# Layer 0's down end reordered, three k/v products placed into it, and half of the row scaling moved from the projection into the attention

## The chip, the cores and the metric

The kernel runs on one core of a Trainium2 chip. The core has a matrix engine (TensorE, PE in the profile; PEld is its weight load), a vector engine (VectorE, DVE), an engine for activations (ScalarE, ACT), a general one (GpSimd, POOL) and one that mostly issues transfers (SyncE, SP). Each works through its own queue of instructions in order; semaphores hold an instruction until what it needs is there. The metric is the device time of one execution in microseconds (us).

## The reference, cut to what matters

A stream of 1024 latent tokens and 256 context tokens of width 1024 goes through two layers, each a mixer and a gated convolutional FFN; after both, `x <- LayerNorm(alpha*x + gate*f)`. Layer 0's FFN ends with a product with w_down; layer 1's mixer is attention in a window of 128 tokens to each side and over the context, with 16 query heads and 2 key/value heads.

```python
def odd_project(h, w_in):
    q, k, v = jnp.split(h @ w_in, [C_Q, C_Q + C_KV], axis=-1)
    return heads(q, C_HEADS), heads(k, C_KV_HEADS), heads(v, C_KV_HEADS)

def odd_mixer(h_lat, h_ctx, w_in, w_out, sink, cos, sin, ctx_out):
    q, k, v = odd_project(h_lat, w_in)
    qc, kc, vc = odd_project(h_ctx, w_in)
    q = apply_rope(q, cos, sin)
    k = apply_rope(k, cos, sin)
    y, yc = window_gqa_sink(q, k, v, qc, kc, vc, sink, ctx_out)
    return y @ w_out, ((yc @ w_out) if ctx_out else None)
```

The layer norm between them is split in the kernel: rows are centred and divided by their deviation at once; gain and bias are folded into the modulation that the projection needs, and are put on the stored rows ("row scaling") later, since only the residual at the mixer's end reads them.

## The kernel before, in words

Products are made in three parts (high times high, high times low, low times high) from operands split into a rounded high part and a rest; `mm3` issues the three matmuls (L401 to L403). `split` makes the parts of a weight: ACT casts (L112), DVE or POOL subtracts (L113).

**The down end** (`ffn2`, then `finish_l` in `run`). The product with w_down for columns 512 to 1023 runs with one PSUM bank (`d0` to `d7`) for each of the eight rows of 128 tokens. The last six of its pairs of inputs (18 matmuls) are done row by row. When row t's bank is complete, DVE multiplies by the gate (`tt`, L2039), adds to `z` (L1977) and takes statistics (L1978, L357); POOL takes the root (`rs`, L359, L360); DVE makes `nmr` (L2778), ACT scales `z` (L2779). One row later come eight transposes of `z` (L384) into `d(t-1)` and `d(t)`, eight evictions on ACT with the modulation (`hst`, L390), and on DVE a cast to the high part and a subtraction for the low one (L395, L396). The order on every engine is the program's there.

**The projection** (`l1_project`). First the k/v columns (256) of the eight rows, then the q columns 0 to 511 (q0 phase) and 512 to 1023 (q1 phase), 24 matmuls each. Between rows of the q0 phase the two context rows are normalised, turned (into `tr` banks, pool `pt1`) and projected. Each q row is rotated (L436, L446 on DVE, L450 on POOL), and two products later turned (L471) and evicted, high by ACT (L461), low by DVE (L462), then stored to `qC0`/`qC1`; k likewise to `kC`. In each q row, `sum_rows` also makes part of the next modulation vectors: a load (`accr`), a split (`ahl`, L321, L322), two matmuls (L325, L326) and an addition (`abr`, L330). And `scale_rows` (L2475 to L2478) scales half a row: SP loads 512 columns of a row of x2 into `xs`, DVE multiplies and adds, POOL issues the store. PE's order is the program's (`manual_pe`); the order on the other engines is set by the scheduler.

**The attention** (`attn_c`). Thirty-two groups of four heads and 128 queries, two units each. A unit makes scores `S` (L762), DVE adds the mask and takes the row bound (L2654), ACT exponentiates (L783), POOL divides (L786) by what DVE inverted (L785); PE turns the result `P` (`T`, L858), ACT and DVE copy it out (L773, L771), and PE multiplies with v (`pv`, L867). A dictionary of side jobs (`side`) runs a job with the loads of a group, such as a piece of w_out (`out_weight`: L1215, L1216).

## Time and profile before

| what | us |
|---|---|
| median of 3 runs | 2911.86 (2909.92 to 2914.53) |
| the profiled execution | 2915.36 |
| its span in the trace | 2913.5 |
| mean granted PE clock in it | 0.979 |
| down product, its last rows | about 1707 to 1756 |
| projection of layer 1 | about 1766 to 1908 |
| attention of layer 1 | 1908 to about 2145 |

The places are read off the timeline, from the start of the span. A row of the timeline gives start, duration, engine, line, operation, output and inputs, and in brackets the idle time of the engine before it and what ended that. A row of the table of windows gives, for a stretch of time, each engine's busy time with its number of instructions, and the granted clock of PE as a share of full speed.

### The profile page before, as it was taken

What the parts mean: (1) busy time and instruction counts of PE and PEld (TensorE: products, weight loads), DVE (VectorE), ACT (ScalarE), POOL (GpSimd) and SP (SyncE); (2) the same over time, 40 slices, a digit from 0 to 9 for tenths busy, and PEclk for the clock granted to TensorE, in tenths of its full rate; (3) what the DMA queues carried; (4) which work ended last, traced back from release to release, by engine and by line L of the source; (5) the groups of instructions that cost most, each with busy time, mean ns of one, the idle gap of its engine ahead of it and who ended that gap; (6) DMA issues with size and microseconds to landing.
All of it is one profiled execution on the core that took longest, in us unless ns stands there. A gap on an engine that the chain in (4) does not pass through costs nothing.

```text
span 2913.5 us, 45188 instructions
## 1 busy us (share of the span) xinstructions
PE 2761.8 (95%) x16596; PEld 2251.1 (77%) x16596; DVE 2139.0 (73%) x3832; ACT 1382.7 (47%) x2598; POOL 691.7 (24%) x968
## 2 busy tenths in 40 slices
PE   6989999999999999999999998989999899999997
PEld 4877777777789987888888877766677788888886
DVE  4876366667588778888877656557778888888778
ACT  3221155567535654455553343257753555555541
POOL 2610143354451000000001013435544011111002
PEclk8999999999999999999999999999999999999999
DMA  8468721033558653333367525732234455555862
GB/s 262 138 186 272 214 66 34 17 104 116 156 154 245 213 177 104 105 118 111 117 218 286 177 80 192 235 105 63 71 119 155 140 173 167 173 166 206 325 218 93
DMA packets 370517, 456.87 MB, mean 157 GB/s; under 512 B 26152, under 2 KB 265032, under 8 KB 368760
## 3 DMA queue, kind: packets, MB, share of 16 engines
q1 hardware_dynamic: 342808, 369.40, 40.5%
q0 software_dynamic: 24592, 82.89, 8.2%
q8 instruction: 130, 2.13, 0.3%
q10 hardware_dynamic: 2896, 1.70, 0.2%
q14 instruction: 91, 0.75, 0.1%
HBM read 337.98 MB, written 115.93 MB: 156 GB/s over the span
## 4 chain that ended last, share of the span: by engine, by line
PE 67%; DVE 10%; issue 10%; DMA 7%; ACT 4%; POOL 1%; SPq 0%; ACTq 0%; DVEq 0%; POOLq 0%
PE q L1704 8%; PE x L1704 7%; PE y L1704 7%; PE S L762 5%; PE v L1704 4%; PE pv L907 3%; PE T L893 3%; PE dy L2365 3%; PE mm L401 3%; PE mm L402 2%; PE mm L403 2%; PE d L401 2%; PE d L402 2%; PE d L403 2%; PE dx L2365 2%
## 5 line engine op out<-in xcount | busy, mean ns | idle before, releaser
L786 POOL TENSOR_SCALAR P<-P,rin 128x640 f32<-128x640 f32 (+3 forms) x288 | 250.9, 876 | 344.3 <-DVE rin L785 321.3
L1678 DVE TENSOR_TENSOR w<-raw,w 128x512 fp32r<-128x512 f32 x308 | 209.6, 694 | 85.6 <-ACT w L1676 85.5
L112 ACT CAST w<-raw 128x512 fp32r<-128x512 f32 x315 | 183.4, 621 | 173.4 <-PE d L403 61.1
L113 DVE TENSOR_TENSOR w<-raw,w 128x512 fp32r<-128x512 f32 x299 | 194.3, 689 | 70.3 <-ACT w L112 68.3
L762 PE MATMUL S<-k,q 64*128 64x256 f32 (+2 forms) x1824 | 192.4, 337 | 17.1 <-DVE nm L2654 8.1
L783 ACT ACTIVATE P<-P,nm 128x641 f32<-128x641 f32 (+4 forms) x208 | 161.3, 777 | 82.5 <-DVE nm L2654 46.7
L1676 ACT CAST w<-raw 128x512 fp32r<-128x512 f32 x308 | 182.1, 621 | 15.1 <-DVE raw L1683 10.1
L762 PEld LDWEIGHTS S<-k,q 64*128 64x128 f32 x1824 | 136.0, 188 | 52.7 <-issue 18.3
L773 ACT COPY PT<-T 128x512 f32<-128x512 f32 (+1 forms) x250 | 134.1, 566 | 77.9 <-PE T L893 75.8
L907 PE MATMUL pv<-PT,v 128*64 128x128 f32 x2016 | 133.4, 280 | 16.7 <-ACT PT L773 14.3
L893 PE MATMUL T<-ident,P 128*128 128x128 f32 x1008 | 136.7, 282 | 6.8 <-POOL P L786 2.3
L907 PEld LDWEIGHTS pv<-PT,v 128*64 128x64 f32 x2016 | 109.3, 138 | 42.6 <-ACT PT L773 23.2
L401 PE MATMUL d<-w,w 128*128 128x512 f32 x352 | 138.0, 392 | 0.0
L402 PE MATMUL d<-w,w 128*128 128x512 f32 x352 | 137.4, 390 | 0.0
L403 PE MATMUL d<-w,w 128*128 128x512 f32 x352 | 137.3, 390 | 0.0
L785 DVE RECIPROCAL rin<-den 128x1 f32<-128x1 f32 x288 | 46.1, 162 | 118.7 <-ACT P L783 116.1
L771 DVE COPY PT<-T 128x512 f32<-128x512 f32 (+1 forms) x166 | 110.4, 666 | 30.6 <-PE T L893 20.5
L893 PEld LDWEIGHTS T<-ident,P 128*128 128x128 f32 x1008 | 110.1, 142 | 27.5 <-issue 14.0
L1704 PE MATMUL q<-T3h,w 128*128 128x512 f32 x352 | 118.6, 398 | 8.0 <-DVE ug L2320 4.3
L2365 PE MATMUL dy<-w,w 128*128 128x512 f32 x528 | 120.8, 390 | 0.2 <-DVE w L113 0.2
L1704 PE MATMUL q<-T2h,w 128*128 128x512 f32 x352 | 115.9, 390 | 2.1 <-ACT q L2302 1.7
L1704 PE MATMUL v<-T0h,w 128*128 128x512 f32 x352 | 116.4, 392 | 0.0
(426 smaller groups left out, 7803.4 us busy)
## 6 DMA issues: line engine op xcount, KB each, us to landing
raw<-in_up_dram SPq DMA_DIRECT2D x132, 512.0 KB
raw<-in_down_dram SPq DMA_DIRECT2D x59, 512.0 KB
raw<-g SPq DMA_DIRECT2D x44, 512.0 KB
raw<-G SPq DMA_DIRECT2D x38, 512.0 KB
araw<-in_ada_w_dram SPq DMA_DIRECT2D x32, 512.0 KB
raw<-in_w_in_dram SPq DMA_DIRECT2D x28, 512.0 KB
g<-cv POOLq DMA_DIRECT2D x22, 512.0 KB, 3.0
G<-go POOLq DMA_DIRECT2D x44, 256.0 KB, 2.7
```

Of the source, the lines that this page charges most:

```text
L112: nc.scalar.copy(hi, s)
L113: (lo_eng or nc.vector).tensor_sub(lo, s, f32(hi))
L401: nc.tensor.matmul(ps, lh, rh, start=first, stop=False)
L402: nc.tensor.matmul(ps, lh, rl, start=False, stop=False)
L403: nc.tensor.matmul(ps, ll, rh, start=False, stop=last)
L762: self.nc.tensor.matmul(outs[a], q[r, x, qs], k[r, y, ks], start=(i == 0), stop=(i == 2))
L786: nc.gpsimd.tensor_scalar(P[:, :n], P[:, :n], rin, 1.0, ALU.mult, ALU.mult)
L893: nc.tensor.transpose(ps[:, s * 128 : (s + 1) * 128], P[a][:, cols[i + x] : cols[i + x] + 128], self.ident,)
L907: nc.tensor.matmul(O[a * HD : (a + 1) * HD], v_of(a, vts[i + x]), pT[:, s * 128 : (s + 1) * 128], start=(i + x == 0), stop=(i + x == m - 1 ...
L1678: nc.vector.tensor_sub(half(i, 1), src[i], f32(half(i, 0)))
L1704: nc.tensor.matmul(ps, w[:, a, s], r[b][:, k], start=first and k + i == 0, stop=k == 3 and i == 2, skip_group_check=True,)
L2365: nc.tensor.matmul(banks[q][t], ga[i][:, a, c], wd[i][:, b], start=q < 2 and f + k == 0, stop=f == HF - 1 and k == 2, skip_group_check=True,)
```

## The change

1. *Down end.* Each row's 18 matmuls are parted in two. Between the halves stand row t-2's transposes and evictions (`turn`), row t-1's scaling (`scale`) and the first cast of t-2; after the row, the second cast and the store of t-2. The k/v weights are loaded and split in the down product (`ahead`). Behind the last row come the k/v product of row 0, the turn of row 6, the k/v products of rows 1 and 2, and the turn of row 7. The three products are copied by ACT into a tile of the ring of weights (`fill`).
2. *Projection.* DVE now follows program order too. Weight subtractions for wq and wq2 go from POOL to DVE, in halves at other places. The pool of transposes has 3 banks (2 before), the accumulator 2 tiles, and what is done behind a product (`late`) is done three products later. The rotation table goes to a longer-lived pool, with a small early one for rows 0 and 1. The context rows' low parts are subtracted by DVE. Row scaling takes only columns 0 to 511, only in the q1 phase, with the load one row ahead into tiles of the weight pool. An exponential is issued early (`warm`). The last q row's transposes are put into the attention (`turn_last`).
3. *Attention.* Columns 512 to 1023 are scaled in eight side jobs, with groups 6, 8, 10, 14, 17, 20, 23 and 25, in rows of the pool of `P`. The pool `csm` lies on the other side of the memory.

```diff
-            late = None
+            ahead(0)
+            F = [None] * NLAT
+            half = 2 * NP - last + last // 2
             for t in range(NLAT):
-                for i in range(2 * NP - last, 2 * NP):
+                if t in (4, 6):
+                    ahead(t // 2 - 1)
+                for i in range(2 * NP - last, half):
+                    mm(i, t, bank[t])
+                if t > 1:
+                    F[t - 2].turn(t - 2)
+                if t > 0:
+                    F[t - 1].scale()
+                if t > 1:
+                    F[t - 2].cast(0)
+                for i in range(half, 2 * NP):
                     mm(i, t, bank[t])
                 tt = self.t(tp2, [128, 512], "tt")
                 nc.vector.tensor_mul(tt, bank[t], gate[:, 512:])
                 add(1, t, tt)
-                norm_t, new = finish(t, z[t], s6[t])
-                if late is not None:
-                    late()
-                norm_t()
-                late = new
-            if late is not None:
-                late()
-
+                F[t] = finish(t, z[t], s6[t])
+                if t > 1:
+                    F[t - 2].cast(1)
+
+            def d(i):
+                return self.t(pd, [128, 512], f"d{i}")
+
+            fill(0, d(0))
+            F[6].turn(2)
+            F[7].scale()
+            F[6].cast(0)
+            F[6].cast(1)
+            fill(1, d(1))
+            fill(2, d(4))
+            F[7].turn(5)
+            F[7].cast(0)
+            F[7].cast(1)
...
+    def scale_rows(self, x, dr, g, b):
+        nc = self.nc
+        nc.vector.tensor_mul(x, x, g)
+        nc.vector.tensor_add(x, x, b)
+        nc.gpsimd.dma_start(dr, x)
...
+                    if h0 and t == NLAT - 1:
+                        q = self.t(self.ring, [128, 2, 512], "w")[:, 0]
+                    else:
+                        q = self.t(st, [128, 512], "q", bufs=3)
                     self.rope(st, ps, 8, rp[:, t, 0:HD], rp[:, t, HD:], q)
-                    scale_rows(t + (NLAT if h0 else 0))
+                    if h0:
+                        load_rows(t + 1)
+                        self.scale_rows(*xs.pop(t), gb["ln_g"], gb["ln_b"])
+                    if h0 and t == NLAT - 1:
+                        return q
...
-                acc = self.t(st, [128, 512], "accr")
+                acc = self.t(st, [128, 512], "accr", bufs=2)
...
+            E = mybir.EngineType
+            with self.tc.manual_schedule(engines={E.PE, E.DVE}):
+                for t in range(3):
+                    late.append(ev_kv(t, kv[t]))
+                for t in range(3, NLAT):
+                    products(t, wkv, 256, ev_kv)
+                    if t in (3, 5):
+                        k0 = 2 * t - 6
+                        wq[k0:] = self.load_in(w, 0, 512, nc.vector, range(k0, k0 + 4))
+                sum_load(0)
                 for t in range(NLAT):
-                    products(t, wkv, 256, ev_kv)
-                    if t == 1:
-                        wq = self.load_in(w, 0, 512, nc.gpsimd)
-                for t in range(NLAT):
-                    s = sum_rows(t)
-                    next(s)
+                    sum_load(t + 1)
                     if t in (2, 3):
                         xc[t - 2] = rows_c(t - 2)
                     products(t, wq, 512, ev_q(0))
                     if t in (3, 4):
                         turn_c(t - 3, xc[t - 3])
-                    next(s)
-                    if t > 0:
-                        for _ in old:
-                            pass
-                    old = s
+                    next(sums[t])
+                    for _ in sums.pop(t - 1, ()):
+                        pass
                     if t == 5:
                         for c in (8, 9):
                             products(c, wkv, 256, ev_kv)
-                        wq2 = self.load_in(w, 512, 512, nc.gpsimd)
+                        wq2 = self.load_in(w, 512, 512, nc.vector, range(4))
+                wq2 += self.load_in(w, 512, 512, nc.vector, range(4, KT))
+                late.pop(0)()
                 self.ckv = {0: self.load_kvC(self.ck, 0)}
+                load_rows(0)
...
+                    if t == 4:
+                        nc.scalar.activation(warm, snk[:, :1], AF.Exp)
+                self.q_last = late.pop()
...
+            def turn_last():
+                ps = self.t(pt, [128, 512], "T").rearrange("p (j t) -> p j t", j=4)
+                for j in range(4):
+                    nc.tensor.transpose(
+                        ps[:, j], self.q_last[:, j * 128 : (j + 1) * 128], self.ident
+                    )
...
+            xs, gb = {}, []
+
+            def x_load(t):
+                if t == 0:
+                    for n in ("ln_g", "ln_b"):
+                        gb.append(self.t(sp, [128, 512], n, bufs=1))
+                        self.bcast(gb[-1], io[n][0, 1, 512:])
+                xs[t] = row(), d["x2"][t * 128 : (t + 1) * 128, 512:]
+                nc.sync.dma_start(*xs[t])
+                self.scale_rows(*xs[t], *gb)
...
+            side = {1: turn_last, 4: lambda: self.out_rows(io["w_out1"], 2)}
...
+            for t, g in enumerate((6, 8, 10, 14, 17, 20, 23, 25)):
+                side[g] = lambda t=t: x_load(t)
...
+        class finish_l:
+
+            def __init__(s, t, z, s6):
+                s.t, s.z = t, z
+                s.mv, s.rs = kern.stats(box["st"], s6)
+
+            def scale(s):
+                nm = kern.t(box["st"], [128, 1], "nmr", bufs=3)
+                nc.vector.tensor_scalar(nm, s.mv[:, 0:1], s.rs, -1.0, ALU.mult, ALU.mult)
+                nc.scalar.activation(s.z, s.z, AF.Identity, bias=nm, scale=s.rs)
+
+            def turn(s, b):
+                s.h = []
+                for q in range(2):
...
+            def cast(s, q):
+                hi, lo = (
+                    v[:, 4 * q : 4 * q + 4, s.t * 128 : (s.t + 1) * 128] for v in H["l"]
+                )
+                nc.vector.tensor_copy(hi, s.h[q])
+                nc.vector.tensor_sub(lo, s.h[q], f32(hi))
+                if q == 1:
+                    nc.sync.dma_start(rows("x2")(s.t), s.z)
+
+        wraw, wkv, kv = [], [], []
+
+        def ahead(i):
+            wv = io["w_in1"].rearrange("(k p) n -> p k n", p=128)
...
+        def fill(t, ps):
...
+            (hi, lo), o = H["l"], t * 128
+            for k in range(KT):
+                self.mm3(ps[:, :256], hi[:, k, o : o + 128], lo[:, k, o : o + 128],
+                         *wkv[k], k == 0, k == KT - 1)
+            nc.scalar.copy(kv[t], ps[:, :256])
```

The number of PE's rows in the program stays 11917. Three places show what moves.

DVE, in the down end around row 5 (`hst` is what ACT evicted from transposes, `tt` the gated product of the row's bank, `nmr` what ACT's scaling of `z` waits for); before:

```order
2107 L395 CAST h1lh_3136_17171<-hst_3172_17406 128x4x128
2108 L396 TENSOR_TENSOR h1ll_3137_17172<-hst_3172_17406,h1lh_3136_17171 128x4x128
2109 L395 CAST h1lh_3136_17171<-hst_3174_17418 128x4x128
2110 L396 TENSOR_TENSOR h1ll_3137_17172<-hst_3174_17418,h1lh_3136_17171 128x4x128
2111 L2778 TENSOR_SCALAR nmr_3175_17426<-mv_3169_17396,rs_3170_17398 128x1
2112 L2039 TENSOR_TENSOR tt_3176_17447<-d5_3057_16555,gate_2896_15580 128x512
2113 L1977 TENSOR_TENSOR z5_2885_15569<-z5_2885_15569,tt_3176_17447 128x512
2114 L1978 BN_STATS s65_2893_15577<-z5_2885_15569 128x6
2115 L357 BN_AGGR mv_3177_17451<-s65_2893_15577 128x2
```

and in the change:

```order
2104 L2883 CAST h1lh_3136_17171<-hst_3173_17384 128x4x128
2105 L2884 TENSOR_TENSOR h1ll_3137_17172<-hst_3173_17384,h1lh_3136_17171 128x4x128
2106 L2857 TENSOR_SCALAR nmr_3182_17448<-mv_3176_17411,rs_3177_17413 128x1
2107 L2883 CAST h1lh_3136_17171<-hst_3179_17429 128x4x128
2108 L2884 TENSOR_TENSOR h1ll_3137_17172<-hst_3179_17429,h1lh_3136_17171 128x4x128
2109 L2052 TENSOR_TENSOR tt_3183_17462<-d5_3057_16555,gate_2896_15580 128x512
2110 L1978 TENSOR_TENSOR z5_2885_15569<-z5_2885_15569,tt_3183_17462 128x512
2111 L1979 BN_STATS s65_2893_15577<-z5_2885_15569 128x6
2112 L357 BN_AGGR mv_3184_17466<-s65_2893_15577 128x2
```

Before, `nmr` of row 4 stands behind both casts and subtractions of row 3's evictions (`hst_3172`, `hst_3174`), with nothing between it and row 5's product. Now it stands behind row 2's second pair and ahead of row 3's first.

ACT, behind the last row; before (`vst` is the first v row):

```order
1302 L390 ACTIVATE hst_3196_17571<-d5_3195_17566,m2ab0_579_3222 128x128 x4
1303 L390 ACTIVATE hst_3198_17583<-d6_3197_17578,m2ab0_579_3222 128x128 x4
1304 L112 CAST w_3242_17769<-raw_3241_17767 128x512
1305 L112 CAST w_3243_17772<-raw_3241_17767 128x512
1306 L2779 ACTIVATE z7_2887_15571<-z7_2887_15571,nmr_3199_17591,rs_3194_17563 128x1024
1307 L390 ACTIVATE hst_3201_17599<-d6_3200_17594,m2ab0_579_3222 128x128 x4
1308 L390 ACTIVATE hst_3203_17611<-d7_3202_17606,m2ab0_579_3222 128x128 x4
1309 L480 COPY vst_3223_17698<-mm_3222_17673 128x128
```

and in the change (`w_3204` holds the products, L112 are casts of wq):

```order
1296 L2909 COPY w_3204_17588<-d0_3203_17587 128x256
1297 L112 CAST w_3249_17832<-raw_3248_17830 128x512
1298 L2873 ACTIVATE hst_3206_17615<-d2_3205_17614,m2ab0_579_3222 128x128 x4
1299 L2873 ACTIVATE hst_3208_17625<-d3_3207_17624,m2ab0_579_3222 128x128 x4
1300 L2858 ACTIVATE z7_2887_15571<-z7_2887_15571,nmr_3209_17634,rs_3202_17581 128x1024
1301 L2909 COPY w_3204_17588<-d1_3210_17642 128x256
1302 L112 CAST w_3250_17835<-raw_3248_17830 128x512
1303 L112 CAST w_3252_17840<-raw_3251_17838 128x512
1304 L112 CAST w_3253_17843<-raw_3251_17838 128x512
1305 L2909 COPY w_3204_17588<-d4_3211_17668 128x256
1306 L2873 ACTIVATE hst_3213_17695<-d5_3212_17694,m2ab0_579_3222 128x128 x4
1307 L2873 ACTIVATE hst_3215_17705<-d6_3214_17704,m2ab0_579_3222 128x128 x4
```

Three copies of k/v products now stand between the evictions of rows 6 and 7, and the first of them ahead of the scaling of `z7`.

DVE, in the q part of the projection; before, where the scheduler set the order (`xs` are row tiles in scaling, `mm` a product's bank):

```order
2192 L2476 TENSOR_TENSOR xs_3408_18648<-xs_3408_18648,ln_g_3291_18061 128x512
2193 L2477 TENSOR_TENSOR xs_3408_18648<-xs_3408_18648,ln_b_3292_18063 128x512
2194 L436 TENSOR_TENSOR rp1_3300_18108<-mm_3298_18082,rp_3214_17650 128x512
2195 L446 TENSOR_TENSOR rp2_3301_18109<-mm_3298_18082,rp_3214_17650 128x16x16 x2
2196 L459 TENSOR_TENSOR qst_3304_18121<-tr_3303_18119,qst_3304_18121 128x128
2197 L322 TENSOR_TENSOR ahl_3305_18126<-accr_3297_18080,ahl_3305_18126 128x512
2198 L330 TENSOR_TENSOR abr_3307_18132<-small_3306_18129,abr_3307_18132 1x512
2199 L2476 TENSOR_TENSOR xs_3422_18711<-xs_3422_18711,ln_g_3420_18707 128x512
```

in the change, at the start of the q1 phase, and then in the attention's group 6:

```order
2238 L437 TENSOR_TENSOR rp1_3415_18673<-mm_3413_18647,rp_3221_17736 128x512
2239 L447 TENSOR_TENSOR rp2_3416_18674<-mm_3413_18647,rp_3221_17736 128x16x16 x2
2240 L2465 TENSOR_TENSOR raw_3412_18645<-raw_3412_18645,ln_g_3410_18641 128x512
2241 L2466 TENSOR_TENSOR raw_3412_18645<-raw_3412_18645,ln_b_3411_18643 128x512
2242 L330 TENSOR_TENSOR abr_3419_18687<-small_3418_18684,abr_3419_18687 1x512
2243 L463 SCALAR_TENSOR_TENSOR qst_3422_18721<-tr_3421_18716,qst_3422_18721 128x512
2244 L437 TENSOR_TENSOR rp1_3424_18727<-mm_3420_18691,rp_3221_17736 128x512
2245 L447 TENSOR_TENSOR rp2_3425_18728<-mm_3420_18691,rp_3221_17736 128x16x16 x2
```

```order
2367 L2725 ISA P_3657_19729,nm_3654_19714<-S_3655_19715,msk_3222_17738,snk_3223_17740 128x512
2368 L2725 ISA nm_3654_19714 128x1
2369 L2465 TENSOR_TENSOR P_3652_19706<-P_3652_19706,ln_g_3650_19702 128x512
2370 L2725 ISA P_3660_19737,nm_3654_19714<-S_3656_19716,msk_3222_17738,snk_3223_17740 128x512
2371 L2725 ISA nm_3654_19714 128x1
2372 L2466 TENSOR_TENSOR P_3652_19706<-P_3652_19706,ln_b_3651_19704 128x512
2373 L786 RECIPROCAL rin_3659_19734<-den_3658_19731 128x1
```

Each row's scaling now stands behind its rotation; in the attention the first pass stands between the two mask passes of a unit and the second behind them, ahead of the inversions.

110 lines of the change are left out of this document (66 added, 44 removed).

## The prediction

> **What bounds the kernel now.** I read the page first: the busy shares and the chain of waits.
>
> ```profile
> PE 2761.8 (95%) x16596; PEld 2251.1 (77%) x16596; DVE 2139.0 (73%) x3832; ACT 1382.7 (47%) x2598; POOL 691.7 (24%) x968
> PE 67%; DVE 10%; issue 10%; DMA 7%; ACT 4%; POOL 1%; SPq 0%; ACTq 0%; DVEq 0%; POOLq 0%
> ```
>
> TensorE (PE) sets the end, and the change neither adds nor removes a matmul. So the time can only move by what PE stands idle and by what it runs at a lower clock. The second view is therefore the table of windows over the stages that the diff touches: last rows of the down product (1705 to 1758 us), the gap behind them, the projection's q part (1800 to 1860), the attention's start (1908 to 1926) and its steady part (1930 to 2145); then the four stretches where the granted clock stood at half.
>
> ```profile
> core 0: us, PE busy (x) PEld busy (x) DVE busy (x) ACT busy (x) POOL busy (x), PEclk, DMA share, GB/s
> 1705.00:1758.00 53.00, 44.09 (x210) 35.09 (x209) 36.08 (x65) 31.24 (x66) 12.42 (x19) 0.97 0.24 90
> 1758.00:1765.00 7.00, 0.72 (x4) 0.67 (x4) 4.46 (x8) 4.91 (x11) 6.29 (x6) 0.57 0.66 225
> 1800.00:1860.00 60.00, 51.83 (x261) 43.29 (x260) 39.46 (x65) 18.66 (x42) 29.27 (x27) 0.94 0.76 239
> 1908.00:1926.00 18.00, 8.59 (x52) 6.36 (x51) 7.78 (x21) 6.32 (x13) 4.81 (x11) 0.63 0.78 196
> 1930.00:2145.00 215.00, 211.52 (x1882) 145.99 (x1881) 154.30 (x426) 157.02 (x369) 114.07 (x243) 1.00 0.19 60
> 1718.00:1721.50 3.50, 2.87 (x9) 2.49 (x10) 1.30 (x3) 2.09 (x6) 0.69 (x2) 0.51 0.14 54
> 1759.00:1769.30 10.30, 4.96 (x23) 4.96 (x24) 5.67 (x12) 6.81 (x16) 5.48 (x6) 0.50 0.69 238
> 1820.50:1827.30 6.80, 4.24 (x12) 3.56 (x13) 6.75 (x11) 1.40 (x4) 3.98 (x4) 0.50 0.76 237
> 1912.60:1926.30 13.70, 6.19 (x31) 4.88 (x32) 5.71 (x16) 5.54 (x11) 3.28 (x8) 0.50 0.86 203
> ```
>
> Idle PE is 53 - 44.09 = 8.9, 7 - 0.72 = 6.3, 60 - 51.83 = 8.2 and 18 - 8.59 = 9.4 us: 32.8 us. Work done at half clock would have taken half as long: 2.87, 4.96, 4.24 and 6.19 us of it cost 1.4, 2.5, 2.1 and 3.1 us, 9.1 in all. Some 42 us are the most that the four places hold. In the attention's steady part only 215 - 211.52 = 3.5 us are idle, but there every other engine is over half busy: that is where a cost can arise.
>
> **Down end, the rows.** Per row PE does 18 matmuls, then 8 transposes.
>
> ```profile
> PE d L384 <- ACT z L2779: 13.6, 7, 6.3
> ...
> 1750.57 1.09 PE L384 MATMUL d<-ident,z 128*128 128x128 f32 x8 [1.09 <-ACT z L2779]
> 1756.97 1.09 PE L384 MATMUL d<-ident,z 128*128 128x128 f32 x8 [1.18 <-ACT z L2779]
> 1764.34 1.97 PE L384 MATMUL d<-ident,z 128*128 128x128 f32 x8 [6.28 <-ACT z L2779]
> ...
> 1749.28 1.24 ACT L2779 ACTIVATE z<-z,nmr,rs 128x1024 f32<-128x1024 f32 x1 [1.35 <-DVE nmr L2778]
> 1751.32 2.91 ACT L390 ACTIVATE hst<-d,m2ab 128x128 f32<-128x128 f32 x8 [0.81 <-PE d L384]
> ...
> 1749.51 0.69 DVE L2039 TENSOR_TENSOR tt<-d,gate 128x512 f32<-128x512 f32 x1 [0.28 <-PE d L403]
> 1755.83 0.69 DVE L2039 TENSOR_TENSOR tt<-d,gate 128x512 f32<-128x512 f32 x1 [0.29 <-PE d L403]
> 1756.55 1.78 DVE L1977 TENSOR_TENSOR z<-z,tt 128x512 f32<-128x512 f32 x1
> ...
> L396 DVE TENSOR_TENSOR h1ll<-hst,h1lh 128x512 fp32r<-128x512 f32 x12 | 8.3, 692 | 0.4
> L395 DVE CAST h1lh<-hst 128x512 fp32r<-128x512 f32 x12 | 5.0, 419 | 6.3 <-ACT hst L390 6.3
> ```
>
> The wait answer's columns are total, times and longest; timeline rows give start and duration. A row takes 1755.83 - 1749.51 = 6.3 us, of which PE idles 1.1 to 1.2 for ACT's z. The row is a loop: 0.81 to the first transposes, evictions 2.91, then ACT stands 1.35 for nmr, which DVE has behind the casts of just these evictions, then z 1.24: 6.3. In the new order nmr stands ahead of those casts and z half a row behind its statistics, so the 1.35 leaves the loop. What is late next? ACT's loop without it: 1.24 + 2.91 + 0.81 = 4.96 us. VectorE (DVE): a product, an add and statistics at 0.69 us each, two casts at 0.42 and two subtractions at 0.69, and two small ones of 0.21, 4.7 in all. PE: 6.3 - 1.1 = 5.2. PE sets the pace, with 0.25 us of room. Two rows carry a weight split each (some 1.4 us on DVE), so they may keep some wait. Of 8.9 idle and 1.4 at half clock I take 9; bounds 4 (three rows keep their full wait, and the first, unlike rows, do too) and 10.3.
>
> **Down end, behind the last row.** Here z7 must pass add, statistics and scaling: 6.28 us of idle, then half clock through the first k/v products. Now three of those products come before the last transposes. What one takes, is read later, at full clock, from the transposes between two of them:
>
> ```profile
> 1776.14 0.27 PE L471 MATMUL tr<-ident,q 128*128 128x128 f32 x1
> 1779.12 0.27 PE L471 MATMUL tr<-ident,q 128*128 128x128 f32 x1
> ```
>
> That is 3.0 us with one transpose. z7 is ready about 8.3 us after the last row, by this trace (1764.3 - 1755.8 = 8.5 with its contended add of 1.78). PE has three products and row 6's transposes, 3 x 3.0 + 1.1 = 10 us, to do first. So the wait is covered with 1.7 us to spare. Since the added instructions are moved, not new, the gain is the idle and the half clock: 6.3 + 2.5 = 8.8. k/v weights must be loaded and split by then; their load is issued before the rows, some 40 us ahead. I take 8; bounds 6.3 and 8.8.
>
> **Projection.** The idle lies in the q part:
>
> ```profile
> PE tr L384 <- DVE qst L462: 7.7, 3, 4.5
> ...
> ACT ahl L321 <- DMA accr<-adp: 6.5, 2, 6.2
> ...
> L2476 DVE TENSOR_TENSOR xs<-xs,ln_g x16: 670/692/1751, 1778.2 to 1845.7; 128x512 f32<-128x512 f32 x16
>   DMA xs<-x: 20.0, 12
> DMA to landing us min/median/max: 2.3/2.7/5.1
> ```
>
> DVE stands 20 us, in 12 waits, for the rows that it scales; a q eviction queued behind them comes late, and PE's transposes of the context rows wait for a bank (4.5 us once). The change takes the scaling out of the q0 phase wholly, loads the rest a row ahead, and adds a third bank. It adds to DVE the 16 weight subtractions that POOL did: 16 x 0.69 = 11 us spread over 130. POOL loses them. DVE's order is now the program's: an instruction that waits (a product of sums waiting for the accumulator's load, 6.2 us here) holds all behind it, rotation and evictions too, and PE then waits for banks. Two-deep accumulator tiles load it a row ahead, against that. At the first q1 row, the last subtractions for wq2 queue behind a q eviction, the rotation and the sums: about 1.4 us of PE wait. With 8.2 + 2.1 = 10.3 at hand I take 8.5; bounds 4 (4.5 us wait gone only) and 10.3.
>
> **Attention's start.**
>
> ```profile
> 1907.56 1.03 PE L471 MATMUL tr<-ident,q 128*128 128x128 f32 x8
> 1917.61 0.75 DVE L2654 CUSTOM_DVE_ANT_0 P<-S,msk,snk 128x512 f32<-128x512 f32 x1 [2.89 <-DMA qC<-qst]
> 1918.51 1.28 ACT L783 ACT_TABLE_LOAD   x1 [4.52 <-DVE nm L2654]
> 1924.80 1.91 PE L858 MATMUL T<-ident,P 128*128 128x128 f32 x9
> ...
> 1907.83 0.69 DVE L436 TENSOR_TENSOR rp<-mm,rp 128x512 f32<-128x512 f32 x1 [3.98 <-PE mm L403]
> 1908.44 0.74 DVE L446 TENSOR_TENSOR rp<-mm,rp 128x256 f32<-128x256 f32 x2
> 1909.10 1.28 DVE L462 SCALAR_TENSOR_TENSOR qst<-tr,qst 128x512 fp32r<-128x512 f32 x2
> ```
>
> From the last product (1907.56) to the first score pass on DVE are 10 us, to the first transposes 17.2. The first pass now waits for no store: the new pools lie elsewhere, the last q row is turned within the attention, and the table load is made earlier. DVE must do the last rotation (0.69 + 0.74), two evictions (1.28) and one row's scaling (two passes, 1.38) first, 4.1 us with nothing waited for; with what POOL and ACT put between I take 5.5 us after the last product. From there to the transposes were 7.2 us, less 1.28 for the table: 5.9. So 11.4 instead of 17.2: 5.8 gained, less something for the last row's turn. I take 5; bounds 2.5 (the pass is held back 3 us by a scaling whose store or load is late) and 9.4 (all idle).
>
> **Scaling in the attention.** Eight jobs, each a load, two DVE passes and a POOL-issued store.
>
> ```profile
> 2015.20:2022.40 7.20, 7.17 (x66) 4.97 (x64) 4.87 (x15) 5.69 (x13) 3.66 (x9) 1.00 0.18 57
> 2022.40:2030.40 8.00, 7.69 (x66) 5.14 (x64) 6.16 (x16) 5.27 (x12) 4.17 (x10) 1.00 0.26 82
> ...
> 2022.07 0.89 DVE L1216 TENSOR_TENSOR w<-P,w 128x512 fp32r<-128x512 f32 x1 [0.54 <-ACT w L1215]
> ```
>
> These are two groups of equal matmul count. The second held a job that already exists, one weight piece's split with one DVE subtraction of 0.89 us: it took 0.8 us longer. So a group has little slack, and a job with two passes (1.4 us, or 2.4 with the first at the maximum of the xs row) costs about as much or more. I take 0.8 each, 6 in all; bounds 1 (they fit where DVE is idle) and 15 (the first pass at its maximum, 1.06 us over the median, in every job: 8 x 1.86).
>
> **Sum.** 9 + 8 + 8.5 + 5 - 6 = 24.5 us. The profiled execution took 2915.36 us: 2890.9. It lies 3.5 above the median of the runs, 2911.86, so on the median's scale the forecast is 2887. All low bounds together would be 4 + 6.3 + 4 + 2.5 - 15 = 1.8, all high ones 10.3 + 8.8 + 10.3 + 9.4 - 1 = 37.8; on the median's scale 2910 and 2874. The low end of the range stands there, since all of the idle and the clock is hardly got at once and more isn't there to get; the high end goes most of the way to the other.
>
> **Rivals.**
> 1. *The rows keep ACT's pace.* ACT's 4.96 leaves 0.25 us; a DVE pass stretched to 1.78, as in the last row, breaks it. For: two split rows. Against: POOL's competing subtractions leave this stage. Eight rows back at 6.3: the 9 shrinks to 1, time 2895.
> 2. *Program order blocks the projection.* For: the 6.2 us accumulator wait; against: its loads come a row earlier. The 8.5 goes: 2896.
> 3. *Slower: the scaling stalls the attention.* DVE's first pass waits at the head for its load (median landing 2.7 us), and the softmax passes behind it wait too. With the load fully exposed and contended passes (1.75 + 0.69), a job costs 2.7 + 2.4 = 5.1 us: 41 us, against 30.5 gained, 2922. It decides from 30.5 / 8 = 3.8 us a job on. Against it: SP's queue has nothing that would hold the load back to its pass.
> 4. *The clock stays whole at the remaining idles.* Half clock followed idles of 0.95 + 1.60 us in the down end (the stretch from 1718). My sum leaves about 3 us of it at the attention's start. Without it: 2884. [...]
> 5. *Every scaling pass is stretched.* L2476's longest pass was 1751 ns against a median of 692; if all first passes in the attention were like it, beside a POOL that is busy 114 of 215 us, 8 x 1.06 = 8.5 us come on top of the 6: 2895. Against: the median stayed at 692 while POOL was busy 29 of 60 us in the q part. [...]
> 6. *It doesn't shorten anything:* the gains up front are taken back at the attention, whose later loads (w_out pieces, q blocks) then set the pace: 2912. Against: DMA share there is 0.19.
>
> **How the numbers follow.** Forecast 0.44, rival 1 0.11, rival 2 0.15, rival 3 0.05, rival 4 0.11, rival 5 0.07, rival 6 0.07. The range 2874 to 2906 takes in rivals 1, 2, 4 and 5 and leaves out 3, 6 and the tails. What this kernel's measurement can tell from no change is 0.2%, 6 us: faster means below 2906. Faster: 0.44 + 0.11 + 0.15 + 0.11 + 0.07 = 0.88, less a tail, 0.86; the same 0.08, rival 6 and a tail; slower 0.06, rival 3 and a tail.
>
> **What would show it.** Right: rows of the down end 5.2 us apart, with no wait on z above 0.5; no idle over 1 us between the last row and the fourth k/v product; clock 1.00 through the down end; about 130 us from the last row to the last q product; transposes of the attention 11 to 12 us behind it; groups with a scaling about 0.8 us longer than their neighbours. Wrong: rows at 6 us or more with ACT or DVE named; PE waiting for DVE over 2 us in the projection; DVE passes of the scaling named with a DMA wait in the attention.

## The result, and the profile after

The changed kernel takes 2889.66 us (median of 4 runs, 2888.20 to 2897.43), the kernel before 2911.97 us beside it (4 runs, 2909.92 to 2914.53). The ratio is 0.9927, with a 95% interval of 0.9914 to 0.9940: 22.3 us less, against 25 forecast from the median. The profiled execution took 2889.54 us with a span of 2887.5. The page, busy shares and chain:

```profile
PE 2753.8 (95%) x16596; PEld 2245.4 (78%) x16596; DVE 2145.7 (74%) x3852; ACT 1381.7 (48%) x2602; POOL 671.6 (23%) x948
PE 67%; DVE 10%; issue 10%; DMA 6%; ACT 4%; POOL 2%; SPq 0%; ACTq 0%; POOLq 0%; DVEq 0%
```

The shares say next to nothing: 67% of the chain is PE before and after. The table of windows over the same stages does:

```profile
core 0: us, PE busy (x) PEld busy (x) DVE busy (x) ACT busy (x) POOL busy (x), PEclk, DMA share, GB/s
1695.00:1748.00 53.00, 53.00 (x311) 46.54 (x310) 37.96 (x79) 36.92 (x83) 9.10 (x17) 1.00 0.32 116
1748.00:1800.00 52.00, 51.86 (x296) 45.07 (x295) 34.20 (x82) 20.13 (x50) 12.57 (x16) 1.00 0.56 168
1800.00:1868.00 68.00, 67.34 (x340) 56.15 (x339) 45.82 (x76) 13.09 (x27) 19.89 (x18) 1.00 0.64 185
1868.00:1884.20 16.20, 10.84 (x63) 8.21 (x63) 11.78 (x27) 7.20 (x18) 6.58 (x13) 0.68 0.95 310
1887.00:2106.00 219.00, 210.27 (x1851) 144.77 (x1850) 162.81 (x436) 154.95 (x361) 119.44 (x248) 1.00 0.31 94
```

From the last rows of the down product to the end of the projection (1695 to 1868 us) PE now idles 0.8 us and the clock is 1.00 throughout. At the attention's start 5.4 us of idle and a clock of 0.68 remain. In the steady attention the idle grew from 3.5 to 8.7 us.

PE's instructions are the same in both programs, so their starts can be laid beside each other. Stretches between the same events, from the two traces:

| stretch | before | after | gain | forecast |
|---|---|---|---|---|
| start of the span to row 0's gated product in the down end | 1711.38 | 1701.46 | 9.9 | none |
| row 0's to row 7's gated product | 44.45 | 34.47 | 10.0 | 9 |
| to the first sums matmul behind the second q product | 46.41 | 35.76 | 10.65 | 8 |
| to the end of the last q product | 105.49 | 95.55 | 9.9 | 8.5 |
| to the third group of the attention | 22.36 | 19.73 | 2.6 | 5 |
| to the end of the attention | 218.50 | 227.19 | -8.7 | -6 |
| to the end of the program | 758.27 | 766.72 | -8.45 | none |

The five stretches with a forecast give 24.5 us, to the tenth what was forecast for their sum. Such closeness is luck: three of the gains were forecast 1.0, 2.65 and 1.4 us too low, the fourth 2.4 too high and the cost 2.7 too low, and these cancel. The first and the last stretch, 9.9 and -8.45, were in no forecast and nearly cancel too; they are taken up below.

The down end's rows, as groups of one tile with minimum, median and maximum duration in ns and the first and last start:

```profile
L2052 DVE TENSOR_TENSOR tt<-d,gate x8: 683/684/692, 1701.5 to 1735.9; 128x512 f32<-128x512 f32 x8
```

Eight in 34.4 us, 5.0 to 5.1 us apart from row 1 on (6.3 in the last rows before).

The attention's start after the change:

```profile
1867.07 1.47 PE L472 MATMUL tr<-ident,q 128*128 128x128 f32 x12
1870.20 0.68 DVE L2465 TENSOR_TENSOR raw<-raw,ln_g 128x512 f32<-128x512 f32 x1
1870.91 1.65 DVE L2466 TENSOR_TENSOR raw<-raw,ln_b 128x512 f32<-128x512 f32 x1
1873.09 0.74 DVE L2725 CUSTOM_DVE_ANT_0 P<-S,msk,snk 128x512 f32<-128x512 f32 x1
1873.65 0.60 ACT L462 ACTIVATE qst<-tr 128x512 fp32r<-128x512 f32 x1 [4.86 <-DMA qC<-qst]
1873.89 0.54 PE L763 MATMUL S<-k,q 64*128 64x256 f32 x1 [2.56 <-DVE nm L2725]
1880.55 3.09 PE L859 MATMUL T<-ident,P 128*128 128x128 f32 x12
```

The first score pass stands 6.0 us behind the last product (10 before), but the first transposes 13.5 us (17.2 before), and twelve of them take 3.1 us, at half clock (0.50 from 1880.5 to 1883.7 us).

A group with a scaling, the eleventh:

```profile
1941.66 0.34 SPq L2671 DMA_DIRECT2D P<-x  x1
...
1945.22 0.69 DVE L2465 TENSOR_TENSOR P<-P,ln_g 128x512 f32<-128x512 f32 x1 [1.16 <-DMA P<-x]
1945.83 0.88 DVE L2725 CUSTOM_DVE_ANT_0 P<-S,msk,snk 128x640 f32<-128x640 f32 x1
1946.63 0.08 DVE L2725 DVE_READ_ACCUMULATOR2_ANT nm<- 128x1 f32 x1
1946.63 0.69 DVE L2466 TENSOR_TENSOR P<-P,ln_b 128x512 f32<-128x512 f32 x1
1947.24 0.88 DVE L2725 CUSTOM_DVE_ANT_0 P<-S,msk,snk 128x640 f32<-128x640 f32 x1
...
1948.18 1.14 PE L763 MATMUL S<-k,q 64*128 64x256 f32 x11 [1.03 <-DVE nm L2725]
```

SP issues the load 3.6 us ahead of the pass that needs it, and DVE stands 1.16 us for it with the mask passes of the unit queued behind; PE then waits 1.03 us for the bound that the second of them gives.

### The profile page after: what moved, and what is told of

The parts are those of the page before. It is cut to its first block, busy times and chain, and to the rows that moved or that the text cites. A ratio compares the mean times of both kernels' runs of the same rounds, so it can differ in the third digit from the quotient of the medians.

```text
span 2887.5 us, 45159 instructions
## 1 busy us (share of the span) xinstructions
PE 2753.8 (95%) x16596; PEld 2245.4 (78%) x16596; DVE 2145.7 (74%) x3852; ACT 1381.7 (48%) x2602; POOL 671.6 (23%) x948
## 4 chain that ended last, share of the span: by engine, by line
PE 67%; DVE 10%; issue 10%; DMA 6%; ACT 4%; POOL 2%; SPq 0%; ACTq 0%; POOLq 0%; DVEq 0%
PE q L1705 7%; PE x L1705 7%; PE y L1705 7%; PE S L763 4%; PE v L1705 4%; PE pv L908 3%; PE T L894 3%; PE mm L402 3%; PE mm L403 3%; PE mm L404 3%; PE d L403 3%; PE d L402 3%; PE d L404 3%; PE dy L2387 3%; PE dx L2387 2%
## 5 line engine op out<-in xcount | busy, mean ns | idle before, releaser
L1679 DVE TENSOR_TENSOR w<-raw,w 128x512 fp32r<-128x512 f32 x308 | 208.6, 691 | 88.3 <-ACT w L1677 88.2
L112 ACT CAST w<-raw 128x512 fp32r<-128x512 f32 x315 | 183.5, 621 | 170.6 <-PE d L404 66.5
L113 DVE TENSOR_TENSOR w<-raw,w 128x512 fp32r<-128x512 f32 x315 | 204.4, 689 | 73.1 <-ACT w L112 71.0
```

The source lines that it names most:

```text
L112: nc.scalar.copy(hi, s)
L113: (lo_eng or nc.vector).tensor_sub(lo, s, f32(hi))
L1679: nc.vector.tensor_sub(half(i, 1), src[i], f32(half(i, 0)))
```

## The experiments

Stretches below are those of the table. Each kernel is the changed one with the edit shown. Twelve further profiles, one of them of the kernel before, had the same stretches within 0.1 us wherever their code there was the same, from row 0 of the down end to the last q product, so that parts of a us can be told there from one profile. (Of the kernel before, rows and projection came out 0.7 us shorter each in its second profile.) The attention's start is not so steady: in the nine profiles whose code there is the change's it takes 17.94 to 20.28 us, so its gain is told from one profile to some 2 us only.

### The eight jobs taken out of the attention

```diff
-            for t, g in enumerate((6, 8, 10, 14, 17, 20, 23, 25)):
-                side[g] = lambda t=t: x_load(t)
```

> The changed kernel without the eight side jobs in the attention: columns 512 to 1023 of x2 stay without gain and bias, so that part of the residual is left out. Theory A (the jobs lengthen their own groups and nothing else): groups 6, 8, 10, 14, 17, 20, 23, 25 come back to the lengths they had before the change (6.8, 7.0, 7.25, 7.25, 7.25, 7.25, 7.25, 6.8 us), about 8.7 us less over groups 2 to 31, all other groups within 0.05 us, and the time is 8 to 9 us under the changed kernel's. Rival B (the jobs only fill idle time, and the longer groups come from the changed start or another memory layout): the groups stay as they are, time within 2 us of the changed kernel's.

2880.10 us; ratio to the kernel before 0.9900 (0.9884 to 0.9917). The third group to the end takes 218.51 us, as before the change (218.50). Lengths of the groups with a job, from one group's first score matmul to the next's, worked out from the three traces:

```
group (from 0)      6     8    10    14    17    20    23    25
before           6.82  6.98  7.25  7.25  7.25  7.24  7.24  6.76
changed          6.98  8.70  8.69  8.36  8.36  8.59  8.36  7.08
without the jobs 6.83  6.98  7.25  7.25  7.25  7.24  7.25  6.76
```

Theory A holds. The jobs cost 8.3 us in their own groups and 0.4 net in the others (group 18, behind a job, is 0.7 longer, group 12 0.2 shorter). They cost 0.16 and 0.32 us in groups 6 and 25, and 1.1 to 1.7 in the others. Those two are groups of the first and last queries, whose units are 512 columns wide instead of 640.

### The old order of rows

```diff
-                (first three pairs; turn of t-2; scaling of t-1; first cast; last three pairs)
+                for i in range(2 * NP - last, 2 * NP):
+                    mm(i, t, bank[t])
...
                 F[t] = finish(t, z[t], s6[t])
+                if t > 0:
+                    F[t - 1].turn(max(t - 2, 0), t - 1)
+                    F[t - 1].cast(0)
+                    F[t - 1].cast(1)
+                F[t].scale()
```

> The changed kernel with the down end's rows in the old order: all 18 matmuls of a row, its statistics, then the turn of the row before with its casts, then the scaling; the three k/v products still stand ahead of the last row's turn. Theory A (the row loop over nmr behind the casts was the cost): rows 6.3 us apart again, ACT waiting 1.35 us a row for nmr, some half clock in the down end, 10 us lost between the product of row 0 and that of row 7; time about 10 us above the changed kernel's. Rival B (the rows gain only from weight splits having left POOL, not from the order): rows stay near 5.1 us, time within 2 us of the changed kernel's.

2901.01 us, ratio 0.9975 (0.9964 to 0.9986): 11.4 us above the changed kernel. Rows 0 to 7 take 43.62 us (34.47), the next stretch 37.92 (35.76). The timeline of PE and of ACT:

```profile
1735.92 1.09 PE L2859 MATMUL d<-ident,z 128*128 128x128 f32 x8 [1.80 <-ACT z L2849]
1742.22 1.09 PE L2859 MATMUL d<-ident,z 128*128 128x128 f32 x8 [1.09 <-ACT z L2849]
...
1740.92 1.24 ACT L2849 ACTIVATE z<-z,nmr,rs 128x1024 f32<-128x1024 f32 x1 [1.35 <-DVE nmr L2848]
```

Row period and the 1.35 us wait are back. (In this run and the next, row 6 is turned within the loop, and row 7 alone behind the three products.) The order of the rows is what gained the 9 to 10 us. What in that order, the next run tells.

### The old order of rows, nmr ahead of the casts

```diff
                 if t > 0:
                     F[t - 1].turn(max(t - 2, 0), t - 1)
+                F[t].scale()
+                if t > 0:
                     F[t - 1].cast(0)
                     F[t - 1].cast(1)
-                F[t].scale()
```

> As old_rows (rows in the old order, 18 matmuls together, turn of the row before behind them), with one thing otherwise: nmr and the scaling of a row stand ahead of the casts of the row before's evictions on DVE. In old_rows the product of row 0 to that of row 7 took 43.6 us, in the change 34.5. Theory A (the loop over nmr behind the casts was the 1.35 us a row, and taking it out of the loop is what the change gained): ACT no longer waits 1.35 us for nmr, rows 5.2 us apart or a little more, 35 to 37 us. Rival B (what matters is that transposes stand in the middle of a row, half a row away from the statistics): rows stay at 5.8 us or more, 41 us or more.

2899.07 us, ratio 0.9960 (0.9947 to 0.9973). Rows 0 to 7 take 41.50 us: 2.1 of the 9.15 come from this, 7.0 do not.

```profile
1725.86 1.09 PE L2860 MATMUL d<-ident,z 128*128 128x128 f32 x8 [1.04 <-ACT z L2850]
1731.51 1.09 PE L2860 MATMUL d<-ident,z 128*128 128x128 f32 x8 [0.43 <-ACT z L2850]
...
1724.56 1.24 ACT L2850 ACTIVATE z<-z,nmr,rs 128x1024 f32<-128x1024 f32 x1 [1.31 <-DVE nmr L2849]
1730.22 1.24 ACT L2850 ACTIVATE z<-z,nmr,rs 128x1024 f32<-128x1024 f32 x1 [0.71 <-DVE nmr L2849]
```

Rows are 5.65 and 6.26 us apart in turn. ACT still waits for nmr, now because the row's own statistics (product, add, statistics, root) have only just been made. Rival B is right for the larger part: the place of the transposes matters more than the casts. The 7.0 us are a remainder, though. The change parts the row, scales half a row later and turns a row two rows behind instead of one, and no run tells these apart.

### No k/v products in the down end

```diff
-            fill(0, d(0))
...
-            fill(1, d(1))
-            fill(2, d(4))
...
+                for t in range(NLAT):
                     products(t, wkv, 256, ev_kv)
```

> The changed kernel with the row order of the change, but no k/v product ahead of the last turn: the three products come first thing in the projection, their weights still loaded and split ahead. Theory A (the gap behind the last row was a wait that only the products cover): PE idles 5.5 to 6.5 us before row 7's transposes, the clock halves for some 10 us, and 8.5 to 10 us are lost between the end of row 7 and the fourth k/v product. Rival B (with nmr ahead of the casts z7 comes early enough): idle under 2 us, no half clock, loss under 2 us.

2901.66 us, ratio 0.9970 (0.9958 to 0.9983): 12 us above the changed kernel. Row 7's product to the first sums takes 43.98 us against 35.76, and rows 0 to 7 take 35.53 against 34.47: 9.3 us. The timeline of PE, a cast on ACT, and the window behind:

```profile
1736.39 1.09 PE L2863 MATMUL d<-ident,z 128*128 128x128 f32 x8 [2.71 <-ACT z L2853]
1741.22 1.97 PE L2863 MATMUL d<-ident,z 128*128 128x128 f32 x8 [3.73 <-ACT z L2853]
...
1731.79 0.62 ACT L112 CAST w<-raw 128x512 fp32r<-128x512 f32 x1 [1.32 <-DMA raw<-in_w_in_dram]
...
1738.90:1745.80 6.90, 4.58 (x22) 4.58 (x23) 3.81 (x8) 5.17 (x13) 0.10 (x1) 0.51 0.56 195
```

The gap is in two parts, 2.71 us before row 6's transposes and 3.73 before row 7's, 6.4 together. Row 6's comes in part from ACT, whose order is the scheduler's in the projection: casts of wq were drawn up into the down end, one of them standing 1.32 us for its load ahead of row 6's scaling. That scaling begins 6.0 us behind row 6's gated product, 4.9 in the changed kernel, so some 1.1 us are the casts'; in the changed kernel the first k/v product stands ahead of row 6's transposes and covers the rest. Row 7's is the wait that the products cover, with the clock at half behind it. Theory A holds, though 1 to 3 us of the loss, by estimate, are the casts'.

### DVE's order in the projection set by the scheduler

```diff
-            with self.tc.manual_schedule(engines={E.PE, E.DVE}):
+            with self.manual_pe():
```

> The changed kernel with DVE's order in the projection set by the scheduler again; PE's stays the program's. Theory A (the early scheduling of row scalings and sums ahead of the evictions was what kept PE waiting, and program order removed it): PE idle in the q part comes back, 3 us or more in all, perhaps with half clock; the stretch from the first k/v product to the last q product 3 to 10 us longer than 121.7 us. Rival B (what counts is that half of the scaling is gone, that loads come a row ahead and that there is a third bank; the order doesn't matter): that stretch within 1 us of 121.7.

2887.46 us, ratio 0.9921 (0.9906 to 0.9936). The two stretches of the projection take 36.88 and 94.20 us, 131.08 together, against 131.31 in the changed kernel. DVE's waits, by engine and cause:

```profile
DVE rp L437 <- PE mm L404: 24.1, 9, 4.5
DVE raw L2465 <- DMA raw<-x: 5.7, 4, 2.3
```

Rival B: in this kernel the order is worth nothing. DVE even waits for row loads here (5.7 us in four), and PE has only one idle of 0.9 us.

### Each row loaded in the slot that scales it

```diff
-                        load_rows(t + 1)
+                        load_rows(t)
...
-                load_rows(0)
```

> The changed kernel with each row of the q1 phase loaded in the slot that scales it, not one ahead, while DVE keeps the program's order. Theory A (in program order a waiting scaling holds back the evictions and rotations behind it, so the load ahead is needed): DVE waits some 2 us a row for the load; PE waits in the q1 phase, 1 us a row or more, and at the attention's start. Rival B (a q1 row has 2 us of DVE to spare and the transposes lag by three products, so the wait is absorbed): q1 phase within 0.5 us, and only the last row's wait shows, 2 us at the attention's start.

2890.07 us, ratio 0.9929 (0.9908 to 0.9949). The projection's stretches, 35.79 and 95.51 us, and the attention's start, 18.94, are the changed kernel's (35.76, 95.55, and 18.90 in its second profile). But the run decides nothing. SP's order is the scheduler's, and it issued the eight loads where it did before: counted from row 7's gated product each stands within 0.15 us of its place in the changed kernel, the last at 127.65 us in both, and DVE waits for none of them. So the loads were not later, and whether a load ahead is needed under DVE's program order stays untested.

### Two banks for the projection's transposes

```diff
-            pt = es.enter_context(self.pool("pt1", bufs=3, space=PSUM))
+            pt = es.enter_context(self.pool("pt1", bufs=2, space=PSUM))
```

> The changed kernel with two banks for the projection's transposes in place of three. Theory A (the third bank was part of what removed the 7.7 us in which PE waited for a q eviction): PE waits for an eviction at the context rows' transposes (8 in a row through two banks), 1 to 5 us more in the q part. Rival B (with the scaling out of the q0 phase the evictions come in time, and the third bank is spare): stretch from the first k/v to the last q product within 0.5 us of 121.7.

2894.78 us, ratio 0.9941 (0.9921 to 0.9960). The q part takes 98.75 us, 3.2 more:

```profile
PE tr L385 <- DVE qst L463: 3.2, 2, 2.2
```

Theory A: of the 7.7 us in which PE waited for a q eviction before the change, 3.2 would still be there with two banks.

### The weight subtractions back on POOL

```diff
-                        wq[k0:] = self.load_in(w, 0, 512, nc.vector, range(k0, k0 + 4))
+                        wq[k0:] = self.load_in(w, 0, 512, nc.gpsimd, range(k0, k0 + 4))
...
```

> The changed kernel with the sixteen subtractions for wq and wq2 back on POOL. Theory A (they took turns with DVE's two-input passes, each 1.2 to 1.5 us there against 0.69, and came late): DVE passes of 1.6 to 1.8 us beside them, PE waits for a weight at the q0 phase's or the q1 phase's start, the stretch from the first k/v product to the last q product 1 to 5 us longer than 121.7. Rival B (DVE's 11 us are missed more than POOL's help hurts): the stretch within 0.7 us of 121.7 or shorter, the 0.66 us wait at the first q1 row gone.

2892.59 us, ratio 0.9934 (0.9919 to 0.9950). The projection's stretches are 37.57 and 95.14 us, 1.4 more together, with other small waits in place of the 0.66 us one:

```profile
PE tr L472 <- POOL q L451: 1.4, 2, 0.9
```

This is theory A's size at its low end, but not its wait: PE waited for no weight, but for the rotation, which POOL does beside the subtractions. All of the loss lies in the first of the two stretches (1.8 us); the second is 0.4 shorter.

### The scaling in the q1 phase, three halves in the attention's shorter groups

In the q1 phase a row's tile holds the first half of row t and the second half of row t-1 (in slot 6 the first half of row 7); the second halves of rows 5, 6 and 7 stay in the attention, loaded a group ahead. Nothing is scaled behind the last q product.

```diff
+                    js = [(t, 0)]
+                    if t == NLAT - 2:
+                        js.append((NLAT - 1, 0))
+                    elif t > 0:
+                        js.append((t - 1, 1))
...
-            for t, g in enumerate((6, 8, 10, 14, 17, 20, 23, 25)):
-                side[g] = lambda t=t: x_load(t)
+            for t, g in ((5, 6), (6, 25), (7, 27)):
+                side[g - 1] = lambda t=t: x_load(t)
+                side[g] = lambda t=t: self.scale_rows(*xs[t], *gb)
```

> The changed kernel with the row scaling put elsewhere: in the q1 phase DVE scales, in rows 0 to 6, the first half of each row and from row 1 to 5 also the second half of the row before (row 6: the first half of row 7); nothing in the last q row; only three second halves (rows 5, 6, 7) are left to the attention, in its shorter groups 6, 25 and 27, each loaded a group ahead. Theory A (DVE has room for it in the q1 rows, 4 to 5 us of 5.9 busy, and the last scaling delays the attention's first pass): attention groups 2 to 31 come back by about 8 us, the attention's first score pass 2 us earlier after the last q product, q1 phase longer by at most 1.5 us; time 7 to 10 us under the changed kernel's. Rival B (passes stretched beside POOL's rotation make a q1 row over 5.9 us of DVE): PE waits in the q1 phase, 1 us a row or more; time the same as the changed kernel's or above.

2885.50 us, ratio 0.9921 (0.9907 to 0.9935). The q part takes 96.45 us (0.9 more), the third group to the end 221.23 (227.19). Groups 24 and 26, not 25 and 27, are longer, by 1.3 us each: with its rows loaded earlier, the scheduler had drawn the two passes into the group before, of 640 columns. DVE's room in the q1 phase was enough.

### The same, loaded in the group that scales

```diff
-                side[g - 1] = lambda t=t: x_load(t)
-                side[g] = lambda t=t: self.scale_rows(*xs[t], *gb)
+                side[g] = lambda t=t: x_load(t)
...
                 nc.sync.dma_start(*xs[t])
+                self.scale_rows(*xs[t], *gb)
```

> As proj_scale, but the three second halves that are left to the attention are loaded in the group that scales them (6, 25, 27). In proj_scale the groups 24 and 26, into which the scheduler had drawn the passes once their rows were loaded earlier, were 1.3 us longer. Theory A (a pass costs nothing in a group of 512 columns and over 1 us in one of 640): groups 24 and 26 at 7.25 and 6.8 us, 6, 25 and 27 longer by 0.5 us at most each, groups 2 to 31 at 219 to 220 us against 227; with the attention's start 2 us earlier and the q1 phase 0.9 longer the time is 7 to 9 us under the changed kernel's on the same chip. Rival B (any job costs 1.1 us wherever it stands): groups 2 to 31 at 222 us, time 5 us under it.

And the changed kernel beside it on the same chip:

> The changed kernel once more, as the measure for the next kernel on the same chip. Its stages should come out as before within 0.1 us from the first row of the down end to the last q product (34.5, 9.6, 26.1, 53.7, 41.8 us), the attention's groups 2 to 31 at 227 us; ratio to the kernel before 0.992 to 0.993. Theory A of the run before this one expects 761 to 768 us behind the attention; rival B 765 to 767.

2880.70 us for this kernel, ratio to the kernel before 0.9896 (0.9882 to 0.9909), against 2889.91 us, 0.9929 (0.9916 to 0.9941) for the change: 9.2 us less. It leaves nothing out and is faster than the kernel before and the changed one. The third group to the end takes 219.06 us (226.54 beside it); groups 24 and 26 are at 7.25 and 6.80, and 6, 25 and 27 longer by 0.2 to 0.4 each, as theory A has it.

The part expected at the attention's start did not come: counted from the end of the last product's matmuls, its first score pass stands at 4.05 us where the change has it at 5.86, yet the third group begins 19.13 us behind it (18.90 and 19.73 in the two profiles of the change; 17.80 in the run before this one). DVE, in this kernel:

```profile
1871.59 0.75 DVE L2738 CUSTOM_DVE_ANT_0 P<-S,msk,snk 128x512 f32<-128x512 f32 x1 [0.40 <-PE S L763]
...
1875.64 0.69 DVE L463 SCALAR_TENSOR_TENSOR qst<-tr,qst 128x512 fp32r<-128x512 f32 x1 [2.63 <-ACT qst L462]
```

What is late next is the eviction of the last q row but one: ACT waits for the store of an earlier one (in the changed kernel 4.86 us for `qC<-qst`), and DVE holds the next score passes behind that eviction.

### The kernel before once more

> The kernel before once more, for its profile. Between the end of the attention and the end of the program the kernel before took 758.3 us and the five profiles of the change and its variants 764.8 to 766.7, though nothing there was changed; and the down product began at 1500.4 us before and at 1488.4 to 1499.0 in the five, whose code up to there is the same. Theory A (both are differences between executions): the stretch behind the attention comes out at some other length, 761 to 768, and the down product's start differs by a few us from 1500.4. Rival B (the change costs 7 us behind the attention): 758.3 again within 1 us.

Its one time is 2906.48 us, its down product begins at 1492.1 us (1500.4), and the stretch behind the attention takes 758.93 us (758.27). In the twelve profiles of the change and its variants, whose code ahead of the down product is the kernel before's, that product begins at 1486.0 to 1499.0 us. So the start of the down product varies by more than 10 us between executions, the second profile of the kernel before lies within the others' range, and the table's 9.9 us can't be put down to the change. Behind the attention rival B is nearer: the twelve profiles have 760.5 to 766.8 us there, the two of the kernel before 758.3 and 758.9.

## Why the prediction was right, point by point

The time came out at 2889.7 us against 2887, and the terms add up to the sum, by errors that cancel. Single steps did not all hold.

**Down end, the rows: right in size, the reason in part.** 10.0 us for 9. PE sets the pace now, at 5.0 to 5.1 us, with no wait for z. The step "nmr stands ahead of those casts, so the 1.35 leaves the loop" carries only 2.1 us of it by the run with that alone; the remaining 7.0 go to the other step, "z half a row behind its statistics", together with the second row of lag before the transposes, which the prediction did not weigh. The two weight splits in rows 4 and 6 cost nothing.

**Behind the last row: right, a little low.** 10.65 us for 8, over the bound of 8.8. The bound left out the 1.18 us in which PE waited ahead of row 6's transposes, which lies behind row 7's product, too; the two stretches together are 20.6 against 17. The run with the subtractions back on POOL loses 1.8 us in this stretch, so some of the 10.65 may be theirs. The run without the three products loses 9.3 us, the larger part of it by the mechanism that was named.

**Projection: right in size, wrong in what was feared.** 9.9 us for 8.5, with one wait of 0.66 us (1.4 expected) at the first q1 row. The fear was DVE's program order (rival 2). The run with a scheduled DVE shows that the order matters neither way; the load ahead was not tested. Of the 9.9 us the third bank is worth 3.2; the subtractions on DVE gained 1.8 in the stretch before and nothing here. The rest, some 6.7, is left for the scaling that is no longer in the q0 phase; no run tested it by itself.

**Attention's start: mis-sized.** 2.6 us for 5 (3.8 between the second profiles). The first pass came as forecast, 6.0 us behind the last product for 5.5. The step that failed is "from there to the transposes 5.9": 7.5 were measured (1873.09 to 1880.55). Behind idles of 1.5 and 2.6 us the clock was at half again (0.50 from 1874.0 to 1884.1 us), and an eviction held by a store stands between the first passes. The two runs that moved the scaling away from there took 17.80 and 19.13 us, so they show no clear gain.

**Scaling in the attention: mis-sized, in the other direction.** 8.7 us for 6. The forecast's 0.8 us for each was one other job's cost; measured were 1.1 in three groups of 640 columns, 1.3 to 1.7 in the three where DVE stands over 1 us for the load, and 0.2 to 0.3 in groups of 512. The sentence in rival 3 that SP's queue has nothing to hold a load back was wrong: the issue stands behind stores that wait for ACT, and DVE waited 4.3 us in four of the eight jobs (and 0.4 in a fifth). That is rival 3's mechanism at a tenth of its price, and one of the signs that the prediction had named for being wrong.

**Stretched passes (rival 5): hardly there.** In the attention the first passes took 673 to 693 ns; the second had a median of 688, with two at 1169, in groups 17 and 23: 1 us in all, against 8.5. See below for where it happened.

**Rival 1 and rival 6** did not come: rows are at 5.0 to 5.1 us. But rival 6's direction, later loads, has a real piece behind the attention. SP's waits there, after and then before:

```profile
SPq L1658 <- DVE w L1217: 8.4, 1, 8.4
```

```profile
SPq L1657 <- DVE w L1216: 0.4, 1, 0.4
```

The second load for layer 1's FFN is held 8.4 us for the place of a weight that DVE is still splitting, until 2.3 us after the attention's end. The loads of y rows stand behind it on SP's queue: the first is issued 4.3 us after that end (3.6 before), its cast begins at 11.8 (10.2), and PE waits for the cast:

```profile
PE o L402 <- ACT yh L1291: 1.4, 1, 1.4
```

In that stretch PE falls 1.7 us behind its place in the kernel before. The rest comes in pieces of up to 3 us within layer 1's FFN, where half clock and waits for casts fall otherwise in each profile (half clock for 3.4 us from 2254.0 and from 2264.2 us before, for 3.4 us from 2232.4 and 6.8 us from 2263.1 us after). That the moved pool (`csm`) or the three more tiles in the ring of weights caused the held load was not tried, and why all twelve lie above the two stays open. It is a cost of 2 to 8 us that the prediction put at nothing.

**The clock (rival 4).** It did not stay whole at the remaining idles: 0.68 in the attention's start, with half clock behind idles of 1.5 and 2.6 us that have 0.9 us of matmuls between them. See below.

## What to carry to other kernels

Read a stage's loop for what separates an operation from its inputs: giving scaling and transposes more distance from a row's statistics was worth three times what reordering the queue behind it was. A side job costs what the group that hosts it lacks: the same two passes cost 0.2 to 0.4 us in a group of 512 columns and 1.1 to 1.7 in one of 640, and five more of them 0.7 to 0.9 us together in the projection; so put it by room, not by pace. When a stall is removed, look past the instruction that waited, since at the attention's start two removed waits gave place to a third.

## What the runs showed of the hardware that was not expected

**Half clock followed the same idle pattern once, and once not.** Windows of the kernel before, around the transposes of the first rows, and then of the kernel with the old order of rows:

```profile
1714.20:1718.70 4.50, 1.95 (x11) 1.17 (x10) 2.59 (x6) 2.75 (x5) 1.25 (x3) 0.93 0.29 117
1718.70:1721.50 2.80, 2.80 (x9) 2.42 (x10) 1.21 (x3) 1.51 (x4) 0.07 (x1) 0.50 0.02 6
```

```profile
1707.00:1711.50 4.50, 1.95 (x11) 1.18 (x9) 2.58 (x6) 2.75 (x5) 1.22 (x3) 1.00 0.29 117
1711.45:1714.50 3.05, 3.05 (x16) 2.58 (x17) 1.89 (x4) 1.51 (x4) 0.13 (x1) 1.00 0.02 5
```

PE was busy 1.95 of 4.5 us with 11 matmuls in both; in the kernel before the idles are of 0.95 and 1.60 us, with four transposes (0.66 us) between them. Then the clock was at half for 3.4 us in the one, and at full in the other. The 2.87 us of work in those 3.4 us would have taken half as long at full clock, by the estimate that the forecast uses too, so the same pattern cost some 1.4 us of clock in the one and none in the other. These windows do not show what made the difference. In the trace of the kernel before, stretches at half clock lasted 3.4 to 17.1 us, in that of the change 3.4 to 10.2 (but for the one in which each trace ends).

**Scaling passes of DVE that began well within a POOL pass on a tensor took 1.17 to 1.67 us, the others 0.67 to 0.69.** In the q1 phase of the last kernel, groups of one instruction with count, total and mean ns; then two passes on DVE and the pass on POOL beside them, from the changed kernel's attention:

```profile
L2466 DVE TENSOR_TENSOR raw<-raw,ln_b 128x512 f32<-128x512 f32 x8 | 12.3, 1543 | 0.3
L2466 DVE TENSOR_TENSOR raw<-raw,accr 128x512 f32<-128x512 f32 x5 | 3.5, 692 | 0.2
```

```profile
1998.00 0.68 DVE L2465 TENSOR_TENSOR P<-P,ln_g 128x512 f32<-128x512 f32 x1
1998.71 1.17 DVE L2466 TENSOR_TENSOR P<-P,ln_b 128x512 f32<-128x512 f32 x1
1998.17 1.16 POOL L787 TENSOR_SCALAR P<-P,rin 128x640 f32<-128x640 f32 x1 [0.29 <-DVE rin L786]
```

In the first fence the pass takes 1.66 us where it begins while POOL's rotation (`q<-rp,rp`, two tensor inputs) is at work, and 0.69 us just behind it (the last of the eight met no rotation, hence the mean of 1.54). In the second, the pass at 1998.00 began ahead of POOL's and kept 0.68 us; the one at 1998.71 began within it and took 1.17, while POOL's took 1.16 for a median of 0.80. Here POOL's second input is one number for each partition, and the DVE pass took 0.5 us more, against 1.0 beside the rotation. In the attention POOL is busy more than half the time (119.44 of 219 us), but of the eight second passes six began with no more than 0.1 us of such a POOL pass left, and stayed at 0.68 to 0.69, so there was little for rival 5 to stretch.
